# Another order of products and of VectorE's and ScalarE's work where the gate and up projections in blocks pass to the down projection

## The chip, the cores and the metric

The kernel runs on one core of a Trainium2 chip. The metric is the time of one execution in device microseconds (us); the value shown for a kernel is the median of its runs. A profile of one further execution gives, for every instruction, engine, start, duration and what it waited for. The engines are named as the profile names them: PE is TensorE, DVE is VectorE, ACT is ScalarE, POOL is GpSimd, SP is SyncE.

## The reference

One inference layer for a prompt of 512 tokens and 8 samples of 8 tokens that share all weights. A mixer (an SSD scan and an mLSTM scan) and a cross attention come first; the last block is the feed-forward part, where the change lies:

```python
u = _rms(x) * g_pre_ffn
f = (jax.nn.silu(u @ w_gate) * (u @ w_up)) @ w_down
x = x + _rms(f) * g_post_ffn
```

All is float32. The width is 1024, the hidden width 2816, that is 22 tiles of 128; the 576 tokens are worked on together.

## The kernel before, in words

**Products of float32 in three.** Every float32 operand is kept as a high part (rounded to a shorter format) and a low part (the rest). A product of 128 by 128 weights with an operand is three matmuls: high by high, high by low, low by high (L1735 to L1737, and L1941, L1942, L1939 for the down projection). The high part is a cast on ScalarE, the low part a subtraction on VectorE, or for some weights a copy with a negative sign on ScalarE and an accumulating transfer on POOL's queue (L1879 and L1880, L1675 and L1676).

**Blocks.** From hidden tile 4 on, gate and up are taken two hidden tiles at a time (class `Pair`, one for gate and one for up), over two halves of the 1024 features and two halves of 288 tokens. That is a 2 by 2 by 2 block product, done with seven block products instead of eight. Block product `w` (0 to 6) multiplies a sum of weight blocks (`factor`) with a sum of input blocks (`b11`, `b21`, `b22`, `parts(1)` to `parts(4)`) in 12 matmuls of 128x288. Products 0, 2, 4 and 5 add up in one PSUM bank `x`, and after each of 0, 2 and 4 the sum so far is copied out by ScalarE before the next is added: to the first half of `cc`, to `ct[:, 0]`, to the second half of `cc` (`c3`). Products 1, 3 and 6 have banks of their own (`y`, `z`), and VectorE adds a copied sum to them. `early` does 0 and 1, `mid` does 2, 3 and 4, `late` does 5 and 6. `done` (L1740) finishes one output block: a gate block gets its SiLU on ScalarE (L1746) behind an addition on VectorE where one is needed (L1745); an up block is multiplied with its gate block (L1750, L1752) and then goes to `place`.

**The operand of the down projection.** The down projection is a block product too (class `Down`, four pairs of output tiles, 0 to 3, in each pass). Its inputs are `hop`, seven combinations of the four hidden blocks `g11`, `g12`, `g21`, `g22`, numbered 0 to 6, each with a high part (cast, L192 or L1770) and a low part (subtraction, L193 or L1773). Three combinations need one block each (0, 1 and 2); the other four come from differences of blocks (`minus`, L1621) when the last block is there.

**The passage.** `down_blocks(c, up_gate, j)` runs twice, for hidden tiles 4 to 9 and 10 to 15. It holds the last gate pair `g_` (products 5 and 6 open), the last up pair `u` and the four `Down` objects. Its list of events `on(t, step)` is sorted by `t`, and that sorted list is the order of instructions on every engine: each engine takes its own instructions one after the other, and an instruction that waits holds those behind it on that engine. Around the passage `u`'s products 0 and 1 come first, then `g_`'s 5 and 6, then `u`'s 2, 3 and 4, then product 0 of `Down` 0, then `u`'s 5 and 6, and then the rest of `Down` 0: products 1, 3, 2 and 5 first for the two older hidden pairs (`(0, 1)`), then for the newest (`(2,)`).

Between them on VectorE and ScalarE stand the weight sums of `Down` 0 and 1: `sum1`, `sum2`, `diff1`, `diff2` on VectorE (L1891 and L1621), `high1` to `high4` as casts (L1885, L1904, L1914, L1922), `low1v` and `low2` to `low4` as subtractions (L1907); `low1` of the third and fourth pair by ScalarE and POOL (L1879, L1880). `keep` copies a down bank to `cc` or `ct` (L1945), `plus` adds it to another on VectorE (L1948), `store` sends rows to memory over POOL's queue (L1954). The matmuls of a down product in the trace read `hop` and weights that are called `whi`, `wlo`, `wacc`, `u3h` or `u3l` after the buffer that they lie in. There are 3 buffers each of `whi` and `wlo`, so a new cast waits for the last product that reads the old weights.

## Time and profile before

| | us |
|---|---|
| median of 3 runs | 1112.37 |
| lowest and highest run | 1111.8 and 1116.81 |
| the profiled execution | 1110.66 |
| its span, first to last instruction | 1108.9 |
| PE busy in the span | 1093.2 |
| DVE, ACT busy in the span | 772.8 and 605.1 |
| first pass through the changed passage | about 839 to 865 of the span |
| second pass | about 942 to 968 |

Times in the views count from the start of the span. A row of the view in order of time has the start, the duration, the engine, the line, the operation, the tile written and the tiles read, and in brackets how long the engine was idle before it and which instruction ended that. A matmul's duration includes its way through the array, so matmuls overlap: distances of their starts show the pace. A row of waits has total, times and longest.

### The profile page before, as it was taken

How to read it: one execution, taken by the hardware profiler on the slowest of the kernel's cores; microseconds unless marked ns; L12 is line 12 of the kernel's file. 1: busy time of each engine (PE TensorE's matmuls, PEld its weight loads, DVE VectorE, ACT ScalarE, POOL GpSimd, SP SyncE). 2: the span in 40 equal slices, each digit the busy share in tenths (PEclk: the TensorE clock that was granted, in tenths of full speed). 3: DMA queues.
4: the chain of work that ended last, by engine and by line, in shares of the span. 5: the costliest groups of instructions: out<-in, count | busy, mean ns of one | idle time of the engine just before them, and what ended most of it. 6: DMA issues, size and time to landing. Idle time of an engine off the chain costs nothing.

```text
span 1108.9 us, 21249 instructions
## 1 busy us (share of the span) xinstructions
PE 1093.2 (99%) x8355; PEld 1041.6 (94%) x8355; DVE 772.8 (70%) x1521; ACT 605.1 (55%) x1122; POOL 217.2 (20%) x301
## 2 busy tenths in 40 slices
PE   9999999999999999999999999999999999999997
PEld 8999889898998999999988889999999999999997
DVE  6796775558785785568744456676578879888655
ACT  6867533246563466656534445635565556556654
POOL 1332542323121121110134301100000210020000
PEclk9999999999999999999999999999999999999999
DMA  6785553435473437873487755652552863397432
GB/s 208 172 155 129 137 160 124 156 84 160 127 207 105 119 136 269 267 257 104 143 271 285 265 184 165 225 183 55 184 147 79 200 163 90 84 240 215 104 135 86
DMA packets 59432, 182.34 MB, mean 164 GB/s; under 512 B 6556, under 2 KB 10780, under 8 KB 58820
## 3 DMA queue, kind: packets, MB, share of 16 engines
q1 hardware_dynamic: 44324, 142.19, 39.1%
q0 software_dynamic: 14720, 38.28, 16.4%
q8 instruction: 65, 1.06, 0.4%
q10 hardware_dynamic: 288, 0.52, 0.1%
q14 instruction: 35, 0.29, 0.1%
HBM read 151.66 MB, written 29.30 MB: 163 GB/s over the span
## 4 chain that ended last, share of the span: by engine, by line
PE 82%; DVE 5%; ACT 4%; DMA 4%; issue 1%; POOL 0%; DVEq 0%; ACTq 0%; SPq 0%; POOLq 0%
PE ps_in L201 5%; PE ps_in L202 5%; PE ps_in L203 5%; PE ps_g L1735 3%; PE ps_g L1736 3%; PE ps_g L1737 3%; PE ps_u L1735 2%; PE ps_u L1736 2%; PE ps_u L1737 2%; PE ps_o L201 2%; PE ps_o L203 2%; PE ps_o L202 2%; PE ps_dn L201 2%; PE ps_dn L203 2%; PE ps_dn L1942 2%; PE ps_dn L202 2%
## 5 line engine op out<-in xcount | busy, mean ns | idle before, releaser
L201 PE MATMUL ps_in<-uh,whi 128*128 128x320 f32 (+1 forms) x544 | 164.5, 303 | 1.4 <-DVE cb L426 1.2
L203 PE MATMUL ps_in<-uh,wlo 128*128 128x320 f32 (+1 forms) x544 | 163.5, 301 | 0.0
L202 PE MATMUL ps_in<-ul,whi 128*128 128x320 f32 (+1 forms) x544 | 163.1, 300 | 0.0
L181 ACT CAST whi<-raw 128x1024 fp32r<-128x1024 f32 (+1 forms) x102 | 102.8, 1012 | 85.3 <-PE ps_in L202 30.1
L188 DVE TENSOR_TENSOR wlo<-raw,whi 128x512 fp32r<-128x512 f32 (+1 forms) x94 | 90.4, 963 | 55.8 <-ACT whi L181 55.1
L201 PEld LDWEIGHTS ps_in<-uh,whi 128*128 128x128 f32 x544 | 103.0, 189 | 4.7 <-issue 1.7
L203 PEld LDWEIGHTS ps_in<-uh,wlo 128*128 128x128 f32 x544 | 103.0, 189 | 1.4 <-issue 0.4
L202 PEld LDWEIGHTS ps_in<-ul,whi 128*128 128x128 f32 x544 | 103.1, 190 | 1.2 <-issue 0.4
L186 POOL DMA_DIRECT2D wlo<-win x32 | 28.0, 885 | 87.5 <-ACT wlo L185 71.5
L1735 PE MATMUL ps_g<-b,whi 128*128 128x288 f32 x144 | 42.7, 297 | 1.2 <-ACT cc L1803 1.0
L1735 PE MATMUL ps_u<-b,whi 128*128 128x288 f32 x144 | 42.8, 297 | 0.0
L1736 PE MATMUL ps_u<-b,whi 128*128 128x288 f32 x144 | 42.5, 295 | 0.0
L1736 PE MATMUL ps_g<-b,whi 128*128 128x288 f32 x144 | 42.5, 295 | 0.0
L201 PE MATMUL ps_o<-mixs_h,whi 128*128 128x320 f32 (+1 forms) x128 | 38.2, 298 | 0.5 <-DVE tmp L991 0.5
L201 PE MATMUL ps_xo<-qh,whi 128*128 128x288 f32 x128 | 37.9, 301 | 0.4 <-ACT whi L181 0.3
L201 PE MATMUL ps_xq<-u2h,whi 128*128 128x320 f32 (+1 forms) x128 | 38.2, 302 | 0.0
L203 PE MATMUL ps_o<-mixm_h,wlo 128*128 128x256 f32 (+1 forms) x128 | 38.2, 298 | 0.0
L202 PE MATMUL ps_xq<-u2l,whi 128*128 128x320 f32 (+1 forms) x128 | 38.0, 298 | 0.0
L201 PE MATMUL ps_o<-mixm_h,whi 128*128 128x256 f32 (+1 forms) x128 | 38.0, 297 | 0.0
L202 PE MATMUL ps_o<-mixm_l,whi 128*128 128x256 f32 (+1 forms) x128 | 37.9, 296 | 0.0
L203 PE MATMUL ps_xq<-u2h,wlo 128*128 128x320 f32 (+1 forms) x128 | 37.9, 296 | 0.0
L202 PE MATMUL ps_o<-mixs_l,whi 128*128 128x320 f32 (+1 forms) x128 | 37.7, 294 | 0.0
(776 smaller groups left out, 3897.7 us busy)
## 6 DMA issues: line engine op xcount, KB each, us to landing
raw<-win SPq DMA_DIRECT2D x35, 512.0 KB, 3.7
raw<-wout SPq DMA_DIRECT2D x17, 512.0 KB, 5.3
kva<-kc SPq DMA_DIRECT2D x16, 512.0 KB, 6.5
kva<-vc SPq DMA_DIRECT2D x16, 512.0 KB, 6.4
raw<-wxq SPq DMA_DIRECT2D x13, 512.0 KB, 3.8
raw<-wgate SPq DMA_DIRECT2D x13, 512.0 KB, 4.4
raw<-wup SPq DMA_DIRECT2D x13, 512.0 KB, 4.3
wlo<-win POOLq DMA_DIRECT2D x24, 256.0 KB, 5.5
```

What stands on the lines that cost most here:

```text
L181: A.copy(hi[:, :n], raw[:, :n])
L186: G.dma_start(lo[:, a:b], src[:, a:b], accum_op=ALU.add)
L188: e.tensor_tensor(lo[:, a:b], raw[:, a:b], hi[:, a:b].bitcast(F32), op=ALU.subtract)
L201: mm(ps, wh, ah, start=i == 0, stop=False)
L202: mm(ps, wh, al, start=False, stop=False)
L203: m = mm(ps, wl, ah, start=False, stop=i == len(tiles) - 1)
L1735: mm(ps, wh, b[0][:, k, :], start=start and k == 0, stop=False, skip_group_check=True)
L1736: mm(ps, wh, b[1][:, k, :], start=False, stop=False, skip_group_check=True)
L1737: m = mm(ps, wl, b[0][:, k, :], start=False, stop=k == 3, skip_group_check=True)
L1942: mm(ps, wh, bl, start=False, stop=False, skip_group_check=True)
```

## The change

Only places change; no arithmetic is added or removed. The product `w = 2` of the last up pair is done between the last gate pair's products 4 and 5 (`up_between`, tied behind product 4 by `issue_after`), not behind 6. The copy of its sum to `ct[:, 0]` is issued inside `done` of the gate block (0, 1), between that block's addition (which reads the old `ct[:, 0]`) and its SiLU; that `done` itself is sorted later, at -3.1, behind `low1v` (-4.2) and `diff1` (-4.1) of `Down` 0. The work behind the up pair's products 5 and 6 is written out in `gate_last` and `place_last`: the gating of block `g21` and its cast come behind product 5 and its low part behind the addition of product 6; the four differences are placed with their casts, and the low parts follow in the order 3, 4, 6, 5. `Down` 0 takes product 5 for the older hidden pairs ahead of product 3 and 1 for the newest, and 3 before 1. `sum2` of `Down` 1 moves from 3.4 to 8.6, `high2` from 8.6 to 8.95, and `low1` of `Down` 2 from 9.6 to 10.5.

```diff
-        def done(s, a, i, ps, more=None):
+        def done(s, a, i, ps, more=None, then=None):
             g = gates(s.j)[a][i]
             if not s.up:
                 if more is not None:
                     V.tensor_tensor(g, ps, more, op=ALU.add)
+                if then:
+                    then()
                 A.activation(g, ps if more is None else g, AF.Silu)
                 return
...
-            s.mul(s.x, 4, parts(3), False)
+            s.m4 = s.mul(s.x, 4, parts(3), False)
...
+        op, ((g11, g12), (g21, g22)) = operand(u.j), gates(u.j)
+        def high(m, g):
+            A.copy(op[:, m, :], g)
+        def low(m, g):
+            V.tensor_tensor(op[:, 7 + m, :], g, op[:, m, :].bitcast(F32), op=ALU.subtract)
+        def gate_last():
+            V.tensor_tensor(g21, g21, u.x, op=ALU.mult)
+            high(1, g21)
+        def place_last():
+            V.tensor_tensor(ct[:, 1, :], u.z, ct[:, 0, :], op=ALU.add)
+            low(1, g21)
+            V.tensor_tensor(g12, g12, ct[:, 1, :], op=ALU.mult)
+            minus(g11, g12, g11)
+            high(3, g11)
+            minus(g12, g22, g12)
+            high(5, g12)
+            low(3, g11)
+            minus(g22, g22, g11)
+            high(4, g22)
+            minus(g21, g21, g22)
+            high(6, g21)
+            low(4, g22)
+            low(6, g21)
+            low(5, g12)
...
-        on(-8.0, up_mul, g_, "x", 5, parts(4), False)
-        on(-6.35, done, g_, 1, 0, "x")
-        on(-6.4, up_mul, g_, "z", 6, b22, False)
-        on(-4.7, lambda: g_.done(0, 1, g_.z, g_.c2))
-        on(-4.8, up_mul, u, "x", 2, parts(2), False)
-        on(-3.15, lambda: A.copy(ct[:, 0, :], u.x))
+        def up_between():
+            with tc.issue_after(g_.m4.ins):
+                up_mul(u, "x", 2, parts(2), False)
+        on(-8.0, up_between)
+        on(-6.4, up_mul, g_, "x", 5, parts(4), False)
+        on(-4.75, done, g_, 1, 0, "x")
+        on(-4.8, up_mul, g_, "z", 6, b22, False)
+        on(-3.1, lambda: g_.done(0, 1, g_.z, g_.c2, lambda: A.copy(ct[:, 0, :], u.x)))
...
-        on(2.9, done, u, 1, 0, "x")
+        on(2.9, gate_last)
...
-        on(4.5, lambda: u.done(0, 1, u.z, ct[:, 0, :]))
+        on(4.5, place_last)
...
-        on(6.8, mul, 0, "y", 1, 1, (2,))
-        on(7.2, mul, 0, "z", 3, 3, (2,))
-        on(7.6, mul, 0, "w", 5, 6, (0, 1), True, False)
+        on(6.8, mul, 0, "w", 5, 6, (0, 1), True, False)
+        on(7.6, mul, 0, "z", 3, 3, (2,))
+        on(8.0, mul, 0, "y", 1, 1, (2,))
...
-        for k, p in (("sum1", 2.3), ("high1", 2.85), ("sum2", 3.4), ("low1v", 8.7), ("high2", 8.6), ("low2", 9.6), ("diff1", 9.7),
+        for k, p in (("sum1", 2.3), ("high1", 2.85), ("sum2", 8.6), ("low1v", 8.7), ("high2", 8.95), ("low2", 9.6), ("diff1", 9.7),
...
-            a_ = ((9.6, 12.2), (18.0, 20.6))[n_ - 2]
+            a_ = ((10.5, 12.2), (18.0, 20.6))[n_ - 2]
```

In the changed kernel the lines from L1746 to the new part of `down_blocks` lie 2 further on (L1907 is L1909 there), and the new functions and events have lines from L2004 to L2054. Three places of the order, in the first pass. The first is TensorE behind the gate pair's product 4 (rows of the change with a +); `b_8940` is where `parts(1)` and `parts(2)` lie, `b_8835` where `parts(3)` and `parts(4)` do:

```order
 L1736 MATMUL ps_g<-b_8835,whi 128x288
 L1737 MATMUL ps_g<-b_8835,u3l 128x288
+L1735 MATMUL ps_u<-b_8940,whi 128x288
+L1736 MATMUL ps_u<-b_8940,whi 128x288
+L1737 MATMUL ps_u<-b_8940,wlo 128x288
```

The three new rows stand four times: the up pair's product 2 now stands between the gate pair's 4 (`u3l`) and 5. The second place is VectorE around the gate block's addition, before:

```order
L193 TENSOR_TENSOR hop_9999<-gt,hop_9999 128x288
L1907 TENSOR_TENSOR wacc<-rawx,wacc 128x768
L1745 TENSOR_TENSOR gt<-ps_g,ct 128x288
L1907 TENSOR_TENSOR wlo<-raw,whi 128x768
L1773 TENSOR_TENSOR hop_9710<-gt,hop_9710 128x288 x2
L1621 TENSOR_TENSOR raw<-raw,sw 128x384
```

and with the change, with ScalarE's rows of the same stretch behind it:

```order
L193 TENSOR_TENSOR hop_9946<-gt,hop_9946 128x288
L1909 TENSOR_TENSOR wacc<-rawx,wacc 128x768
L1909 TENSOR_TENSOR wlo<-raw,whi 128x768
L1775 TENSOR_TENSOR hop_9710<-gt,hop_9710 128x288 x2
L1621 TENSOR_TENSOR raw<-raw,sw 128x384
L1745 TENSOR_TENSOR gt<-ps_g,ct 128x288
```

```order
L1772 CAST hop_9710<-gt 128x288
L1887 CAST whi<-raw 128x768
L192 CAST hop_9946<-gt 128x288
L1916 CAST wacc<-rawx 128x768
L1748 ACTIVATE gt<-ps_g 128x288
L1772 CAST hop_9710<-gt 128x288 x2
L2046 COPY ct<-ps_u 128x288
L1748 ACTIVATE gt<-gt 128x288
L1924 CAST u3h<-raw 128x3x128
```

On VectorE the addition L1745 now stands behind `wlo` (`low1v`), two `hop` rows and `raw` (`diff1`). On ScalarE one `hop` cast has moved ahead of `whi` and one SiLU behind `wacc`, and the copy to `ct` (L2046) stands ahead of the last SiLU. The third place is VectorE from the gating of block `g21` on, before:

```order
L1752 TENSOR_TENSOR gt<-gt,ps_u 128x288
L193 TENSOR_TENSOR hop_9999<-gt,hop_9999 128x288
L1621 TENSOR_TENSOR sw<-sw,raw 128x384
L1750 TENSOR_TENSOR ct<-ps_u,ct 128x288
L1752 TENSOR_TENSOR gt<-gt,ct 128x288
L1621 TENSOR_TENSOR gt<-gt 128x288 x2
L1773 TENSOR_TENSOR hop_9999<-gt,hop_9999 128x288
```

and with the change:

```order
L2013 TENSOR_TENSOR gt<-gt,ps_u 128x288
L2017 TENSOR_TENSOR ct<-ps_u,ct 128x288
L2010 TENSOR_TENSOR hop_9946<-gt,hop_9946 128x288
L2019 TENSOR_TENSOR gt<-gt,ct 128x288
L1621 TENSOR_TENSOR gt<-gt 128x288 x2
L2010 TENSOR_TENSOR hop_9946<-gt,hop_9946 128x288
L1621 TENSOR_TENSOR gt<-gt 128x288 x2
L2010 TENSOR_TENSOR hop_9946<-gt,hop_9946 128x288 x3
L1621 TENSOR_TENSOR sw<-sw,raw 128x384
L1909 TENSOR_TENSOR wlo<-raw,whi 128x768
```

The low part of combination 1 (the `hop` row) has gone behind the addition L2017, the differences stand two and two, and `sw` (`sum2` of `Down` 1) stands behind the last low part.

## The prediction

> **What bounds the kernel now.** I read the page's busy shares first, then TensorE's list of waits, then TensorE's instructions in order of time through the stretch that the change touches, then the chain of waits there. The first fence holds the span, TensorE's busy row, and two rows of TensorE's waits (total us, times, longest).

> ```profile
> span 1108.9 us, 21249 instructions
> PE 1093.2 (99%) x8355; PEld 1041.6 (94%) x8355; DVE 772.8 (70%) x1521; ACT 605.1 (55%) x1122; POOL 217.2 (20%) x301
> ...
> PE ps_g L1735 <- ACT cc L1803: 1.0, 2, 0.5
> PE ps_dn L1941 <- ACT hop L1770: 0.8, 2, 0.4
> ```

> TensorE is busy all the time, so an edit of order can only win what TensorE waits. Both rows say "2 times": the two passes through `down_blocks` look alike, and I work out the first and double it. TensorE's own rows there (start, duration, line, [idle before <- who ended it]):

> ```profile
> 840.76 0.29 PE L1737 MATMUL ps_g<-b,u3l 128*128 128x288 f32 x1
> 841.53 0.40 PE L1735 MATMUL ps_g<-b,whi 128*128 128x288 f32 x1 [0.49 <-ACT cc L1803]
> 841.77 0.30 PE L1736 MATMUL ps_g<-b,whi 128*128 128x288 f32 x1
> ...
> 842.97 0.29 PE L1736 MATMUL ps_g<-b,whi 128*128 128x288 f32 x1
> ...
> 843.23 0.29 PE L1735 MATMUL ps_g<-u3h 128*128 128x288 f32 x1
> ...
> 844.81 0.29 PE L1735 MATMUL ps_u<-b,whi 128*128 128x288 f32 x1
> ...
> 848.01 0.40 PE L1735 MATMUL ps_u<-b,whi 128*128 128x288 f32 x1
> ...
> 850.89 0.40 PE L1735 MATMUL ps_u<-b,whi 128*128 128x288 f32 x1
> ...
> 854.16 0.29 PE L1941 MATMUL ps_dn<-hop,whi 128*128 128x288 f32 x1
> ...
> 856.80 0.29 PE L1939 MATMUL ps_dn<-hop,wlo 128*128 128x288 f32 x1
> 857.49 0.40 PE L1941 MATMUL ps_dn<-hop,whi 128*128 128x288 f32 x1 [0.40 <-ACT hop L1770]
> ...
> 861.08 0.29 PE L1941 MATMUL ps_dn<-hop,wacc 128*128 128x288 f32 x1
> ```

> A product of 12 matmuls takes 844.81 - 843.23 = 1.58, so starts are 0.132 apart. Against that pace: 840.76 to 841.77 holds two steps, 1.01 - 0.26 = 0.75 lost. The starts at 848.01 and 850.89 also show 0.40 instead of 0.29, about 0.1 lost each. From 856.80 to 861.08 there are 19 steps, 4.28 - 2.50 = 1.78 lost. Sum **2.7 per pass, 5.5 in both**: the ceiling of any gain is 0.5%.

> The chain of waits (start, its time on the chain, engine, tile, line) tells who is late in the second stall:

> ```profile
> 844.47 0.33 ACT hop L192
> 844.80 0.31 ACT gt L1746
> 845.11 0.73 ACT wacc L1914
> 845.86 0.96 DVE wacc L1907
> 846.82 0.37 DVE gt L1745
> 847.19 0.87 DVE wlo L1907
> 848.05 0.74 DVE hop L1773 x2
> 848.79 0.48 DVE raw L1621
> ...
> 855.62 0.38 DVE ct L1750
> ...
> 857.47 0.47 DVE hop L1773
> ```

> From 845.86 on it is VectorE's queue: TensorE finished the up pair's last product near 854.2, VectorE took it up (L1750) only at 855.6.

> **First stall: removed.** The change puts the up pair's product 2 between the gate pair's 4 and 5, so ScalarE's copy of `cc` is covered. Product 2 goes from 840.89 to 842.47, with its inputs long there. Product 5 runs 842.47 to 844.05, product 6 to 845.63, the up pair's 3 to 847.21. The 0.75 is won, and TensorE arrives at the up pair's product 4 at **847.21** instead of 848.01.

> **What product 4 waits for: the new stall.** Product 4 adds into the bank that must first be copied to `ct`. That copy is now issued behind the gate pair's last addition (L1745), which reads the same part of `ct`. In VectorE's order L1745 has gone from before the weight difference `wlo` to behind `wlo`, two `hop` differences and `raw`. The head of that queue moves as well:

> ```profile
> 843.30 0.84 ACT L1885 CAST whi<-raw 128x768 fp32r<-128x768 f32 x1 [0.52 <-PE ps_g L1736]
> ...
> 845.01 0.82 ACT L1914 CAST wacc<-rawx 128x768 fp32r<-128x768 f32 x1
> ...
> 847.57 0.38 ACT L2012 COPY ct<-ps_u 128x288 f32<-128x288 f32 x1
> ```

> ScalarE's cast `whi` starts 0.33 after the last high product of 5 (842.97), whose weight buffer it takes. That product is now at 842.47 + 1.33 = 843.80, so `whi` starts at 844.13. Before, `wacc` came 1.71 later with three short operations between; now one stands between (two of about 0.32 moved), so 1.07 later: 845.20, done 846.02. VectorE then, with the chain's pieces: `wacc` 846.06, `wlo` 847.02, two `hop` 847.89, `raw` 848.63, L1745 at 849.1, done 849.5; the copy (0.38) is done 849.9; product 4 starts at **849.95**. Cost: 849.95 - 847.21 = 2.7 idle and 0.1 of a slow restart. The term is 0.2 smaller if `wacc` starts as early as before (845.86); its other bound, no wait at all, is rival A. Queued behind the copy on ScalarE: the SiLU of gate part (0,1), then the casts `u3h` and `whi`, which VectorE waits for; their lateness is in what follows. SP's order is untouched: its two loads behind `u3l` go out about 1 later, and their first reader, ScalarE's `wlo`, is itself 4 later (rival B).

> **Second stall: mostly gone.** From product 4 to the up pair's 5 is 850.89 - 848.01 = 2.88, so 852.83; here the copy of the bank is covered by the down product, and the 0.1 is saved. From 5 to the down products, 854.16 - 850.89 less 0.11 = 3.16: **855.99**, 1.83 later than before. VectorE now finds the last up product when it ends: with 0.3 from a last matmul to its reader, the addition that was at 855.53 to 855.62 is at 856.15, only 0.6 later. `low(1)` goes into the 0.5 that VectorE spent waiting for its own result, about 0.4 more. The differences then come near 857.4, 857.85, 858.65, 859.1, with casts 0.45 behind each; the lows of 3, 4, 6 and 5 are done near 858.75, 860.05, 860.5 and 860.9. TensorE now has 24 matmuls on the two older operands first (the old order had 18, and then needed parts 1 and 3): 855.99 + 3.16 = 859.15 before it needs part 3, which is there, and part 4 at about 859.9, 0.1 to 0.2 short. I take 0.35 with restarts, in place of 1.78; it lies between 0.1 and 0.8 (one more VectorE operation late).

> **Third: a stall that is not there now.** `sum2` of the second down pair (128x384, on VectorE at 855.06 now) moves behind the last low, to about 860.8. All that hangs on it follows late:

> ```profile
> 862.01 0.56 DVE L1621 TENSOR_TENSOR raw<-raw,sw 128x384 f32<-128x384 f32 x1
> ...
> 863.02 0.71 ACT L1945 COPY cc<-ps_dn 128x288 f32<-128x288 f32 x2
> ...
> 863.44 0.82 DVE L1948 TENSOR_TENSOR fst<-cc,ps_dn 128x288 f32<-128x288 f32 x2 [0.88 <-ACT cc L1945]
> ...
> 864.26 0.30 PE L1941 MATMUL ps_dn<-hop,u3h 128*128 128x288 f32 x1
> ```

> The product at 864.26 reuses the bank that the VectorE addition at 863.44 (done 863.9) reads: 0.37 to spare. After the change: `sum2` done 861.35, ScalarE's cast 862.2, its difference on VectorE 863.45, `raw` 863.95 (now 862.57), the cast `u3h` 864.45, the copy `cc` 864.8, the addition done 865.3. TensorE gets there at 864.26 + 0.35 = 864.6. So 0.65 and a restart: **0.75**; from below 0 (if the copy to `cc` does not have to sit behind `u3h`), from above 1.5 (1.4 later, `raw`'s own shift).

> **Sum.** After: 2.8 + 0.35 + 0.75 = 3.9 lost a pass, now 2.7: **+1.2 a pass, +2.4 in both**. The profiled execution took 1110.66 (span 1108.9 and 1.76 around it), so 1113.1; the median shown is 1112.37, 1.7 above that execution, so 1114.8 on its scale.

> **Rivals.** *A, product 4 is not held:* VectorE reaches L1745 before 847.2. Then only the restarts, 0.35 and nothing later remain of 2.7: -2.3 a pass, 1107.7. For it: TensorE's first stall surely goes. Against: in this trace L1745 ran at 846.82 with `wlo`, `hop` and `raw` (2.1) still behind it, and these are ahead of it now; I see no slack. 5%.

> *B, a late transfer; the slower side.* ScalarE's `wlo` (L1879) moves behind the late copy of `cc`, from 860.4 to 864.7, and POOL's accumulating load of the third down pair's weights waits for it, with a store queued behind it on POOL.

> ```profile
> 861.57 0.86 POOL L1880 DMA_DIRECT2D wlo<-wdown  x1 [23.43 <-ACT wlo L1879]
> ...
> DMA to landing us min/median/max: 4.9/5.6/6.3
> ...
> 870.98 0.56 PE L1939 MATMUL ps_dn<-hop,wlo 128*128 128x288 f32 x3
> ...
> f_d<-gt POOLq DMA_DIRECT2D x3, 288.0 KB, 7.8
> ```

> Issue would be at 865.85, landing at 870.75 to 872.15; it is needed at 870.98 + 1.2 = 872.2. Up to 6.3 it is hidden; with the 7.8 that POOL's stores show, it is 1.45 late: +2.65 a pass, 1117.7, and 0.15 more makes it slower by half a per cent. It decides from 6.35 us on. 9%.

> *C, the clock.* A stall of 2.7 is longer than any here; if the granted clock halved after it, product 4 and the down product behind it (2.88) would take twice that: +4.1 a pass, 1120.6. The longest wait of now, and the next four us:

> ```profile
> 355.87 0.64 PE L911 MATMUL ps_nh<-c,qpad 128*32 128x257 f32 x8 [1.68 <-DMA c<-c]
> ...
> 356.40:360.40 4.00, 4.00 (x36) 3.96 (x33) 3.83 (x11) 0.62 (x3) 0.68 (x1) 1.00 0.75 185
> ```

> After 1.68 idle the clock column still reads 1.00, so I give it 3%. [...]

> **How the numbers follow.** The forecast has 83%: 1114.8. Its own range, from the ends above, is +0.2 (third stall absent, `wacc` early) to +2.4 a pass (third at 1.5, second at 0.8), 1112.8 to 1117.2. Runs of one kernel differ here by some us (1111.8 to 1116.81), and B lies just above, so 1110.5 to 1118.3; A and C are left out. Half a per cent, about what a measurement of this kernel can tell from no change, is 5.6: even A is not faster by that much. Faster 2%, same 88%, slower 10% (half of B, C, and the forecast's upper edge).

> **What would show it.** In the changed profile: no wait of L1735 for the `cc` copy at the gate pair's product 5; instead L1735 of the up pair waiting over 2 us for ScalarE's copy of `ct`, with L1745 just ahead on VectorE, twice. The waits of down products for ScalarE's `hop` cast gone or under 0.2. A wait of some 0.6 in front of the down product with `u3h`, for VectorE's addition. If product 4 starts by 848, the sum is wrong by 2 a pass and A holds; if TensorE waits for POOL's load of `wlo`, B; a clock under 0.95 in the slice behind the stall, C.

## The result and the profile after

| | before | after |
|---|---|---|
| median of 15 runs each, taken side by side (us) | 1115.29 | 1120.29 |
| lowest and highest run | 1111.8 and 1120.38 | 1117.04 and 1125.55 |
| ratio after to before, 95% interval | | 1.0057 [1.0045, 1.007] |
| span of the profiled execution | 1108.9 | 1120.2 |
| mean granted clock of TensorE in it | 0.998 | 0.994 |

The change made the kernel slower by 0.57%, about 6.3 us. The forecast was 2.4 us more. The two profiled executions differ by 11.3 us, but 4.3 of that lie ahead of the changed passage (the up pair's product 3 issues its last matmul at 851.36 instead of the 847.08 that the forecast's working gives; a stretch with the granted clock at 0.50 from 356.8 on is part of it), so I compare stretches and not spans.

TensorE's list of waits in the changed kernel (total us, times, longest) has the stall that was forecast, and two smaller ones:

```profile
PE ps_u L1735 <- ACT ct L2046: 5.2, 2, 2.6
...
PE ps_dn L1941 <- DMA wlo<-wdown: 0.8, 1, 0.8
...
PE ps_dn L1943 <- DVE fst L1950: 0.6, 2, 0.3
```

The waits for `cc` at the gate pair's product 5 and for ScalarE's `hop` cast are gone. The chain of waits ahead of the first row is the one that was worked out: the weight difference `wlo`, two `hop` rows and `raw` ahead of the addition L1745, and the copy behind it.

```profile
849.56 0.75 ACT wacc L1916
...
851.20 0.95 DVE wlo L1909
852.15 0.74 DVE hop L1775 x2
852.89 0.47 DVE raw L1621
853.36 0.38 DVE gt L1745
...
853.82 0.41 ACT ct L2046
...
854.27 0.40 PE ps_u L1735
```

What was not worked out stands in TensorE's own rows behind that wait (start, duration, line, what is multiplied):

```profile
851.36 0.29 PE L1737 MATMUL ps_u<-b,wlo 128*128 128x288 f32 x1
854.27 0.40 PE L1735 MATMUL ps_u<-b,whi 128*128 128x288 f32 x1 [2.61 <-ACT ct L2046]
854.50 0.29 PE L1736 MATMUL ps_u<-b,whi 128*128 128x288 f32 x1
...
855.17 0.44 PE L1735 MATMUL ps_u<-b,whi 128*128 128x288 f32 x1
855.40 0.45 PE L1736 MATMUL ps_u<-b,whi 128*128 128x288 f32 x1
855.64 0.45 PE L1737 MATMUL ps_u<-b,u3l 128*128 128x288 f32 x1
...
858.69 0.29 PE L1735 MATMUL ps_u<-b,whi 128*128 128x288 f32 x1
```

851.36 to 854.50 holds two steps of 0.132, so 2.88 are lost, as forecast (2.8). But from 855.17 on, a matmul takes 0.45 instead of 0.29 and starts are 0.24 apart. From 855.17 to 858.69 there are 15 steps: 3.52 instead of 1.98, **1.54 lost with nothing to wait for**. The view by stretches (length, then busy time and instructions of TensorE, its weight loads, VectorE, ScalarE and GpSimd, then granted clock, DMA share, GB/s) says why, in both passes:

```profile
851.80:855.20 3.40, 0.93 (x7) 0.93 (x8) 2.14 (x6) 1.38 (x4) 0.00 (x0) 0.99 0.00 0
855.20:858.60 3.40, 3.40 (x17) 3.40 (x16) 2.22 (x4) 1.17 (x3) 0.00 (x0) 0.50 0.60 181
858.60:862.00 3.40, 3.40 (x28) 3.40 (x28) 1.38 (x3) 1.71 (x4) 0.00 (x0) 1.00 0.13 51
...
957.50:960.90 3.40, 0.88 (x6) 0.89 (x7) 2.14 (x6) 1.34 (x4) 0.00 (x0) 1.00 0.00 0
960.90:964.30 3.40, 3.40 (x17) 3.40 (x16) 2.27 (x4) 1.25 (x3) 0.00 (x0) 0.51 0.56 174
```

The clock is 0.50 for one stretch of 3.4 us behind each wait: 17 matmuls where the next stretch holds 28. That is rival C. The second and third stall:

```profile
865.80 0.29 PE L1943 MATMUL ps_dn<-hop,whi 128*128 128x288 f32 x1
866.08 0.40 PE L1944 MATMUL ps_dn<-hop,whi 128*128 128x288 f32 x1
...
867.16 0.40 PE L1943 MATMUL ps_dn<-hop,wacc 128*128 128x288 f32 x1
867.40 0.29 PE L1944 MATMUL ps_dn<-hop,wacc 128*128 128x288 f32 x1
...
870.71 0.29 PE L1941 MATMUL ps_dn<-hop,wlo 128*128 128x288 f32 x1
871.31 0.40 PE L1943 MATMUL ps_dn<-hop,u3h 128*128 128x288 f32 x1 [0.31 <-DVE fst L1950]
871.55 0.29 PE L1944 MATMUL ps_dn<-hop,u3h 128*128 128x288 f32 x1
```

865.80 to 867.40 holds seven steps, 1.60 - 0.92 = 0.68 lost (forecast 0.35); 870.71 to 871.55 holds two, 0.84 - 0.26 = 0.58 (forecast 0.75). What the second stall is made of stands in the rows of the weight loads (PEld):

```profile
866.08 0.19 PEld L1944 LDWEIGHTS ps_dn<-hop,whi 128*128 128x128 f32 x1 [0.21 <-DVE hop L2010]
...
867.16 0.19 PEld L1943 LDWEIGHTS ps_dn<-hop,wacc 128*128 128x128 f32 x1 [0.29 <-ACT ct L1947]
```

By the steps up to 866.81, 0.35 are lost where TensorE waits for VectorE's low parts, as forecast; the other 0.33, at 867.16 and the start behind it, come from ScalarE's copy of a down bank (L1947, `keep`), which the forecast did not have. So a pass loses 2.88 + 0.68 + 0.58 = 4.1 in stalls (forecast 3.9) and 1.54 in the clock, against 2.7 before: +2.9 a pass. Twice that is 5.9, and the wait for the transfer of `wlo`, which came in the second pass alone, makes it some 6.9 in this execution; 6.3 were measured over the runs.

### The profile page after: what moved, and what is told of

Its sections match the earlier page's. It is cut to its first block, busy times and chain, and to the rows that moved or that the text cites. A ratio compares the mean times of both kernels' runs of the same rounds, so it can differ in the third digit from the quotient of the medians.

```text
span 1120.2 us, 21251 instructions
## 1 busy us (share of the span) xinstructions
PE 1097.5 (98%) x8355; PEld 1045.7 (93%) x8355; DVE 773.0 (69%) x1521; ACT 605.1 (54%) x1122; POOL 216.8 (19%) x301
## 3 DMA queue, kind: packets, MB, share of 16 engines
q8 instruction: 65, 1.06, 0.4%
## 4 chain that ended last, share of the span: by engine, by line
PE 74%; DMA 8%; DVE 5%; ACT 5%; issue 3%; POOL 1%; DVEq 0%; ACTq 0%; POOLq 0%; SPq 0%
PE ps_in L201 5%; PE ps_in L202 5%; PE ps_in L203 5%; PE ps_u L1735 3%; PE ps_u L1736 3%; PE ps_u L1737 3%; PE ps_g L1735 3%; PE ps_g L1736 3%; PE ps_g L1737 3%; PE ps_v L774 2%; PE ps_v L772 2%; PE ps_v L773 2%; PE ps_dn L201 2%; PE ps_dn L203 2%; PE ps_dn L202 2%
## 5 line engine op out<-in xcount | busy, mean ns | idle before, releaser
L1735 PE MATMUL ps_u<-b,whi 128*128 128x288 f32 x144 | 43.2, 300 | 5.2 <-ACT ct L2046 5.2
L1736 PE MATMUL ps_u<-b,whi 128*128 128x288 f32 x144 | 43.1, 300 | 0.0
L1735 PE MATMUL ps_g<-b,whi 128*128 128x288 f32 x144 | 42.5, 296 | 0.2 <-ACT cc L1794 0.2
L1736 PE MATMUL ps_g<-b,whi 128*128 128x288 f32 x144 | 42.5, 295 | 0.0
L202 PE MATMUL ps_xo<-ql,whi 128*128 128x288 f32 x128 | 37.7, 295 | 0.0
```

What stands on the lines that cost most here:

```text
L202: mm(ps, wh, al, start=False, stop=False)
L1735: mm(ps, wh, b[0][:, k, :], start=start and k == 0, stop=False, skip_group_check=True)
L1736: mm(ps, wh, b[1][:, k, :], start=False, stop=False, skip_group_check=True)
```

## The experiments

Every ratio is to the kernel before, from runs side by side on the same chip. The word "pass" is as in the prediction; "lost" is time beyond 0.132 per start on TensorE.

**1. Fill the wait.** The changed kernel, with 18 products ahead of the up pair's product 4 whose results are thrown away. TensorE still gets to product 4 when the copy is done, but is busy until then.

```diff
+        def fill():
+            bank(0, "w")
+            for _ in range(18):
+                mm(ds[0].w, b11[0][:, 0, 0:128], b11[0][:, 0, :], start=True, stop=True, skip_group_check=True)
+        on(-1.65, fill)
```

> The changed kernel with 18 extra matmuls of 128x288, whose results are thrown away, in front of the up pair's product 4 in both passes. They fill the wait for the copy of ct with TensorE work and leave every wait as it is. Theory (the long idle stretch makes the granted clock drop, and the half clock after it is what was not in the forecast): no slice at half clock behind the wait, product 4 starts where it did, and the kernel is 1.4 us a pass, some 2.9 us in all, faster than the changed kernel; against the kernel before it is still 2.5 to 3.5 us slower. Rival (the clock is not tied to this wait, or the missing time lies elsewhere): the clock drops all the same and the time is that of the changed kernel, 5 to 6.5 us slower than before.

Measured: 1.0014 [1.0005, 1.0022], against 1.0057 [1.0045, 1.007]. TensorE's rows (18 throw-away matmuls, then product 4):

```profile
849.09 2.53 PE L2051 MATMUL ps_dn<-u3h 128*128 128x288 f32 x18
...
851.86 0.40 PE L1735 MATMUL ps_u<-b,whi 128*128 128x288 f32 x1 [0.24 <-ACT ct L2046]
```

and the stretch behind them, with 31 matmuls and the clock at 1.00:

```profile
852.00:856.00 4.00, 4.00 (x31) 4.00 (x32) 2.71 (x5) 2.42 (x6) 0.00 (x0) 1.00 0.43 135
```

Counted from the last matmul of product 3, product 4 starts as late as without the filling (2.9 in both), yet the kernel is 0.43% (4.8 us) faster; between the ends of the two intervals, 2.6 to 7.2. The two half-clock stretches are worth 3.1 and the transfer of `wlo`, which was not late here, 1.0. So the clock is the larger part of what the forecast lacked.

That does not rest on the profiled executions alone, since every run has its mean granted clock on record. Over the 15 runs of the changed kernel it is 0.9957 on average, over the 11 of this experiment 0.9984, and over the 23 runs of the kernel before beside them 0.9984 too. One stretch of 3.41 us at half clock, as from 855.16 to 858.58 and from 960.98 to 964.39 in the profiled execution of the changed kernel, takes 0.0015 off the mean of a run. So the changed kernel has some 1.8 such stretches more in a run, at 1.54 each 2.7 us. Its two fastest runs (1117.04 and 1117.13) are the two with the highest clock, 0.998.

What the stalls alone cost is then 1.0014, 1.6 us (0.6 to 2.5 by the interval), where the forecast said 2.4. The expectation, 2.5 to 3.5 slower than before, was missed: the rows of this execution lose 1.4 a pass more than before, 2.8 in both, and why the runs show less is open.

**2. Put the addition back.** The changed kernel with one number undone: the gate block's addition with the copy behind it goes ahead of `wlo` again.

```diff
-        on(-3.1, lambda: g_.done(0, 1, g_.z, g_.c2, lambda: A.copy(ct[:, 0, :], u.x)))
+        on(-4.7, lambda: g_.done(0, 1, g_.z, g_.c2, lambda: A.copy(ct[:, 0, :], u.x)))
```

> The changed kernel with one number put back: the last gate block's addition, with the copy of ct behind it, is sorted at -4.7 again, ahead of low1v and diff1 on VectorE. Theory (this place alone makes the 2.6 us wait, and with it the clock drop): product 4 waits 0.6 instead of 2.6 in both passes, no half clock behind it, and the kernel is 5.5 to 7 us faster than the changed kernel; against the kernel before it is between 1 us faster and 0.5 us slower, because the wait of some 0.5 in front of the down product that reads u3h stays. Rival (the wait has another root, such as the later whi cast on ScalarE): product 4 still waits over 1.5 us, and the clock drops in some of the passes.

Measured: 0.9998 [0.9984, 1.0013]. TensorE's waits in the first pass:

```profile
851.81 0.40 PE L1735 MATMUL ps_u<-b,whi 128*128 128x288 f32 x1 [0.54 <-ACT ct L2046]
855.03 0.40 PE L1735 MATMUL ps_u<-b,whi 128*128 128x288 f32 x1 [0.16 <-ACT cc L2049]
```

The 2.61 has become 0.54 and the clock stays at 1.00 in both passes: with this one number put back, the time can't be told from that of the kernel before.

**3. Put `sum2` back.** The changed kernel with `sum2`, `high2` and `low1` in their old places.

```diff
-        for k, p in (("sum1", 2.3), ("high1", 2.85), ("sum2", 8.6), ("low1v", 8.7), ("high2", 8.95), ...
+        for k, p in (("sum1", 2.3), ("high1", 2.85), ("sum2", 3.4), ("low1v", 8.7), ("high2", 8.6), ...
-            a_ = ((10.5, 12.2), (18.0, 20.6))[n_ - 2]
+            a_ = ((9.6, 12.2), (18.0, 20.6))[n_ - 2]
```

> The changed kernel with sum2, high2 and low1 at their old numbers (3.4, 8.6, 9.6). Theory (these set the wait in front of the down product that reads u3h, and the late transfer of wlo from POOL's queue): both waits go, 0.5 us a pass and up to 0.8 us for the transfer, 1 to 2 us in all against the changed kernel, and the 2.6 us wait and the half clock stay. Against the kernel before 4 to 5 us slower. Rival (these waits are only passed on): the same time as the changed kernel, with a new wait at the down products for ScalarE or VectorE.

Measured: 1.0047 [1.0033, 1.0062]. The waits for L1950 and for the transfer of `wlo` are gone, the one for `ct` is still 5.2 in two, and both stretches at a clock of 0.50 are there (from 855.23 and 961.04). The third stall is gone from the rows, but the 1.1 us between this ratio and that of the change are within the noise of both, so the runs don't show what it is worth. It is not the cause of the loss.

**4. How long must a wait be?** The kernel before, with a measuring stretch behind its end: 40 casts on ScalarE of eight lengths in turn, each of which TensorE waits for and then issues 66 to 86 matmuls of 128x288. None of it enters the output.

```diff
+    lens = (800, 1240, 1680, 2100, 2540, 2970, 3400, 4050)
+        for n_ in range(40):
+            A.copy(dst[:, 0:lens[n_ % 8]], src[:, 0:lens[n_ % 8]])
+            ps = GP("ps_map")[:, :288]
+            for _ in range(66 + 5 * (n_ // 8)):
+                mm(ps, dst[:, 0:128], dst[:, 0:288], start=True, stop=True, skip_group_check=True)
```

> The kernel before with a measuring stretch behind its end: 40 times a ScalarE copy that TensorE must wait for, of eight lengths from 800 to 4050 columns (TensorE idle for about 1 to 4 us), each followed by 66 to 86 matmuls of 128x288 without a pause. The stretch adds work, so only its rows are read, not the time. Theory (the clock is judged in fixed stretches of some 3.4 us that run freely, and one with too little work is followed by one at half clock): idle times of 1.8 us and less never halve the clock, 2.6 us does so in some or most cases by where the stretch falls, over 3.4 us always; each half-clock part is about 3.4 us long whatever the idle time. Rival (a fixed idle time sets it off, and the slow part starts with the first matmul): one sharp bound between 1.7 and 2.6 us and slow matmuls from the restart on.

TensorE's rows, one for each wait: start, time of the group of matmuls, their number, the wait. The third round (76 matmuls: 10.28 at full clock) and three rows of the fifth (86: 11.59):

```profile
1317.69 10.28 PE L2324 MATMUL ps_map<-hl 128*128 128x288 f32 x76 [1.37 <-ACT hl L2321]
1329.70 10.27 PE L2324 MATMUL ps_map<-hl 128*128 128x288 f32 x76 [1.74 <-ACT hl L2321]
1342.06 11.81 PE L2324 MATMUL ps_map<-hl 128*128 128x288 f32 x76 [2.08 <-ACT hl L2321]
1356.32 11.81 PE L2324 MATMUL ps_map<-hl 128*128 128x288 f32 x76 [2.45 <-ACT hl L2321]
1370.94 12.97 PE L2324 MATMUL ps_map<-hl 128*128 128x288 f32 x76 [2.81 <-ACT hl L2321]
1387.08 11.82 PE L2324 MATMUL ps_map<-hl 128*128 128x288 f32 x76 [3.17 <-ACT hl L2321]
...
1569.10 11.59 PE L2324 MATMUL ps_map<-hl 128*128 128x288 f32 x86 [2.08 <-ACT hl L2321]
1583.14 11.60 PE L2324 MATMUL ps_map<-hl 128*128 128x288 f32 x86 [2.45 <-ACT hl L2321]
...
1613.84 11.59 PE L2324 MATMUL ps_map<-hl 128*128 128x288 f32 x86 [3.17 <-ACT hl L2321]
```

A drop cost 1.54 here (11.81 for 10.27), whatever the wait, or less where its stretch began before the matmuls did, and more only where two half-clock stretches followed each other (12.97 for 10.27, 2.7). Over all rounds: none of 14 waits of 1.00 to 1.74 dropped the clock, 2 of 5 of 2.08, 4 of 5 each of 2.45, 2.81 and 3.17, and all 5 of 3.71. Length alone didn't decide: 2.45 and 3.17 stand there both ways. The starts of the drops lie on one grid with a period of 3.413 us: the first at 1151.65, the last at 1629.52, 140 periods of 3.4133 apart, and those between on it to 0.01 us. I call one period a cell. If each wait is cut at that grid, the largest piece in one cell parts the cases cleanly: 20 waits with at most 1.78 in one cell left the clock up, 19 with 1.91 or more dropped it (the expectations of experiment 6 give these counts as 16 and 22; that was a miscount). So in this execution, among dense matmuls of 128x288, every wait that left 1.91 us or more of one cell empty was followed by a cell at half clock, and none that left at most 1.78.

**5. Leave half the wait.** As experiment 1, with 8 throw-away products, so that a wait of 1.56 stays, which is under the 1.78 of experiment 4 wherever the cells lie.

```diff
-            for _ in range(18):
+            for _ in range(8):
```

> The changed kernel with 8 throw-away matmuls of 128x288 (into the bank that the first down product clears afterwards) ahead of the up pair's product 4, where the run before had 18. They take about 1.06 of the 2.6 us that TensorE waits there, so about 1.5 us of idle time stay, in one piece. The arithmetic that counts is that of the changed kernel. Theory (the clock halves only where a stretch of 3.4 us holds more than about 2 us of idle time): no half clock behind product 4 in either pass, matmul starts 0.132 apart, and the time of the kernel with 18 (ratio to before 1.0005 to 1.0022). Rival 1 (any idle time of some length there does it, or the fill hid something else than the clock): half clock behind product 4 as in the changed kernel, ratio near 1.0057. Rival 2 (it depends on where the free-running stretch lies): one pass halves and the other not, ratio near 1.003.

```profile
849.80 1.21 PE L2051 MATMUL ps_dn<-u3h 128*128 128x288 f32 x8
852.57 0.40 PE L1735 MATMUL ps_u<-b,whi 128*128 128x288 f32 x1 [1.56 <-ACT ct L2046]
```

Both passes have this wait, and the profile shows a clock of 1.00 behind both. The mean granted clock over the 12 runs is 0.9981, against 0.9957 for the change and 0.9986 for the 35 runs of the kernel before beside them, so the half-clock cells are absent from most runs too. The time is 1.0027 [1.001, 1.0044]. That is above the range expected (1.0005 to 1.0022), though the interval is wide and overlaps with that of experiment 1; where the difference comes from is open.

**6. The same wait, at known places in the cells.** Three executions of the changed kernel with eight waits of 3.7 behind its end, whose drops mark the grid; the second has 3 throw-away products, which leave 2.21 of the wait, and the third has 72 matmuls behind each marker. The casts and products behind the end enter no output; each of the three is one execution, and their times are not compared.

```diff
+    lens = (4050,) * 8
+        for n_ in range(8):
+            A.copy(dst[:, 0:lens[n_ % 8]], src[:, 0:lens[n_ % 8]])
+            ps = GP("ps_map")[:, :288]
+            for _ in range(66 + 5 * (n_ // 8)):
+                mm(ps, dst[:, 0:128], dst[:, 0:288], start=True, stop=True, skip_group_check=True)
```

> The changed kernel with eight waits of 3.7 us behind its end (a ScalarE cast of 4050 columns that TensorE waits for, then 66 matmuls of 128x288 whose result is thrown away). Each of them is meant to drop the clock, so that the starts of the half-clock stretches show where the free-running stretches of 3.413 us lie in this execution. Theory (the clock halves for the next stretch where one stretch holds more than about 1.85 us in which TensorE has nothing to do: in the measuring stretch all 16 waits with at most 1.78 us in one stretch left it up, all 22 with at least 1.91 dropped it): counted back from the markers, in each of the two passes the wait of 2.61 at the up pair's product 4 drops the clock if at least 1.91 of it lie in one stretch, and leaves it up if at most 1.78 do; over all places, about 7 in 10. Rival (the length of the wait alone decides, and 2.6 always drops it): half clock in both passes wherever the stretches lie.

> As the run before, with 3 throw-away matmuls of 128x288 ahead of the up pair's product 4, so that about 2.2 us of wait stay in one piece. Theory: at least 1.91 in one stretch of 3.413 drops the clock, at most 1.78 leaves it up (over all places about 4 in 10 drop). Rival (the length alone decides): both passes alike, with or without a drop, wherever the stretches lie.

> As the first of these three, with 72 matmuls behind each marker instead of 66: another execution, in which the stretches lie elsewhere. Theory and rival as there: what lies in one stretch decides in each pass, against half clock in both passes.

In each of the three executions the half-clock stretches of the passes and of the markers fit one grid of 3.413 us, and the three grids lie differently (edges at 855.68, 853.30 and 854.08). The second is the telling one. Both passes wait 2.21:

```profile
853.71 0.40 PE L1735 MATMUL ps_u<-b,whi 128*128 128x288 f32 x1 [2.21 <-ACT ct L2046]
957.81 0.40 PE L1735 MATMUL ps_u<-b,whi 128*128 128x288 f32 x1 [2.21 <-ACT ct L2046]
```

The stretches of the next view are cells of the grid, for each pass the one with the wait and the one behind it:

```profile
849.89:853.30 3.41, 1.61 (x13) 1.37 (x11) 3.28 (x6) 0.84 (x4) 0.00 (x0) 1.00 0.00 0
853.30:856.71 3.41, 3.00 (x22) 3.00 (x23) 2.06 (x4) 2.24 (x5) 0.00 (x0) 1.00 0.20 29
955.70:959.11 3.41, 1.30 (x10) 1.30 (x11) 2.13 (x5) 1.75 (x4) 0.00 (x0) 1.00 0.00 0
959.11:962.52 3.41, 3.41 (x17) 3.41 (x16) 2.41 (x5) 1.27 (x4) 0.00 (x0) 0.50 0.69 213
```

In the first pass the cell's edge at 853.30 cuts the wait (851.50 to 853.71) into 1.80 and 0.41: no drop. In the second all of 955.70 to 957.81, 2.11, lies in one cell: half clock. In the two others the pieces are 2.10, 1.92, 2.61 and 2.61, and all four passes dropped. The rival, that length alone decides, has fallen. Behind the markers a second cell stayed at half clock where 0.68 us (the first execution) or more of the wait reached into it, but not with 0.57 (the second) or less. A wait of 2.61 that fills more than 1.91 of one cell leaves at most 0.70 for the next, and in none of the nine passes at half clock on record did a second cell follow.

**7. The products alone.** The kernel before with the up pair's product 2 between the gate pair's 4 and 5, the addition and copy in their old place on VectorE, the tail as before.

```diff
...
+        on(-8.0, up_between)
+        on(-6.4, up_mul, g_, "x", 5, parts(4), False)
+        on(-4.75, done, g_, 1, 0, "x")
+        on(-4.8, up_mul, g_, "z", 6, b22, False)
+        on(-4.7, lambda: g_.done(0, 1, g_.z, g_.c2, lambda: A.copy(ct[:, 0, :], u.x)))
```

> The kernel before with the first part of the change alone: the up pair's product 2 between the gate pair's products 4 and 5, with the copy of its sum behind the addition of block (0, 1), which stays where it was on VectorE (ahead of the weight difference and the two hop rows). The tail behind the up pair's products 5 and 6 and the weight sums stay as before. Theory (what TensorE wins at the gate pair's product 5 it gives back at the first down products, since VectorE's queue sets their start): the 0.75 at product 5 is gone, product 4 waits 0.5 to 0.8 for the copy to ct, the wait of the down products for ScalarE's hop cast stays near 1.8: 0 to +0.5 a pass, ratio 0.999 to 1.001. Rival (the order of products is a gain by itself, and only the later addition spoils it): 0.75 a pass faster, ratio 0.9985 or less.

Measured: 1.0003 [0.999, 1.0016].

```profile
854.30 0.40 PE L1735 MATMUL ps_u<-b,whi 128*128 128x288 f32 x1 [0.54 <-ACT ct L2017]
857.52 0.40 PE L1735 MATMUL ps_u<-b,whi 128*128 128x288 f32 x1 [0.17 <-ACT cc L2020]
864.13 0.40 PE L1943 MATMUL ps_dn<-hop,whi 128*128 128x288 f32 x1 [0.40 <-ACT hop L1772]
```

The 0.75 at the gate product comes back at the up products (1.0 more lost there than before), and the down products wait for `hop` as before: in this order VectorE and ScalarE set the pace through the passage, and an earlier TensorE waits for them further on. The rival's gain (0.9985 or less) lies outside the interval.

**8. The tail alone.** The kernel before with the new order behind the up pair's products 5 and 6 (`gate_last`, `place_last`, the first down pair's products 5, 3, 1), all else as before.

```diff
...
+        on(2.9, gate_last)
...
+        on(4.5, place_last)
...
+        on(6.8, mul, 0, "w", 5, 6, (0, 1), True, False)
+        on(7.6, mul, 0, "z", 3, 3, (2,))
+        on(8.0, mul, 0, "y", 1, 1, (2,))
```

> The kernel before with the last part of the change alone: gating of block g21, differences and low parts in the new order and the first down pair's products 5, 3 and 1 in the new order; the up pair's product 2, the addition of block (0, 1) and the weight sums (sum2, high2, low1) stay as before. Theory: the first stall (0.75 and restarts) stays, the second falls from 1.78 to 0.5 to 0.9 a pass, no third: 0.8 to 1.2 a pass less, ratio 0.998 to 0.999. Rival (VectorE is short of time there whatever the order, so the stall moves on to a later down product): within 0.3 a pass of before, ratio 0.9995 to 1.0005.

Measured: 0.9992 [0.9976, 1.0007]. Counted over all of a pass, as here and in the next two, 2.1 are lost instead of 2.8 (2.7 at the three places of the prediction): the second stall falls from 1.78 to 0.9, the first is there as before. That is the theory's direction, a little less than its 0.8 to 1.2, and the time can't be told from no change.

**9. What each part can give.** The changed kernel with gate product 6 directly behind 5, the addition ahead of `wacc` on VectorE, and `sum2`, `high2` and `low1` in their old places.

```diff
-        on(-4.75, done, g_, 1, 0, "x")
-        on(-4.8, up_mul, g_, "z", 6, b22, False)
-        on(-3.1, lambda: g_.done(0, 1, g_.z, g_.c2, lambda: A.copy(ct[:, 0, :], u.x)))
+        on(-5.58, done, g_, 1, 0, "x")
+        on(-5.6, up_mul, g_, "z", 6, b22, False)
+        on(-5.55, lambda: g_.done(0, 1, g_.z, g_.c2, lambda: A.copy(ct[:, 0, :], u.x)))
...
```

> The changed kernel with two of its numbers undone and one step moved earlier: the gate pair's product 6 stands directly behind product 5, the addition of block (0, 1) with the copy to ct stands ahead of the weight difference wacc on VectorE, and sum2, high2 and low1 have their places of before. It is meant to keep what each part can give: no stall at gate product 5, none or under 0.3 at the up pair's product 4, a second stall of 0.5 to 0.9, no third. Theory (the parts add up): 1 to 2 a pass less than before, ratio 0.996 to 0.9985. Rival (VectorE's queue sets the start of the down products, so an earlier TensorE only waits longer there): the second stall grows to 1.5 or more, ratio 0.9985 to 1.0005.

Measured: 0.9989 [0.9976, 1.0001], which can't be told from no change. A pass loses 2.1 instead of 2.8, so the theory's 1 to 2 less was missed, and the time lies in the rival's range. But the rival's mechanism isn't there either: the second stall is 0.9 and not 1.5. Product 4 no longer waits; what was not expected is a wait of product 5, with ScalarE's queue ahead of it showing its cause:

```profile
852.60 0.83 ACT L1906 CAST whi<-sw 128x768 fp32r<-128x768 f32 x1
853.33 0.39 ACT L2049 COPY cc<-ps_u 128x288 f32<-128x288 f32 x1
...
853.78 0.40 PE L1735 MATMUL ps_u<-b,whi 128*128 128x288 f32 x1 [0.53 <-ACT cc L2049]
```

The copy that the up pair's product 5 waits for stands behind a cast that nothing needs before the down products.

**10. The copy ahead of the cast.** Experiment 9 with that copy ahead of `whi`, block (1, 1)'s two VectorE operations ahead of `wlo`, and the block's low part behind it.

```diff
-        on(0.02, lambda: A.copy(c3, u.x))
-        on(0.1, done, u, 1, 1, "z", c3)
+        def gate_22():
+            V.tensor_tensor(ct[:, 1, :], u.z, c3, op=ALU.add)
+            V.tensor_tensor(g22, g22, ct[:, 1, :], op=ALU.mult)
+            high(2, g22)
+        on(-1.55, lambda: A.copy(c3, u.x))
+        on(-0.75, gate_22)
+        on(-0.65, low, 2, g22)
```

> The kernel of the run before (gate product 6 directly behind 5, the addition of block (0, 1) ahead of wacc, weight sums in their old places) with one more move: ScalarE's copy of the second half of cc stands ahead of the cast whi, VectorE's two operations of block (1, 1) stand ahead of the weight difference wlo and the low part of that block behind it. In the run before, the up pair's product 5 waited 0.53 for that copy (0.80 lost a pass) behind the cast of 0.83. Theory: that wait goes, and since VectorE's queue moves up by as much (the block's two operations no longer stand behind wlo), the second stall stays near 1.0: 0.7 a pass less, 1.4 in all, ratio to before 0.9965 to 0.9985. Rival (VectorE's queue sets the start of the down products whatever TensorE does before): the second stall grows by what the first lost, ratio as in the run before, 0.9976 to 1.0001.

Measured: **0.9969 [0.9955, 0.9982]**, faster than before by 3.5 us, and by the two ratios some 10 less than the change. A pass loses 1.3 instead of 2.8; no wait of over 0.25 is left in it. What remains is the second stall, at 0.76, in part VectorE's low parts and in part ScalarE's copy of a down bank (L1947).

## Why the prediction was wrong, point by point

The step that failed is the clock: the prediction left it out of its sum, at 3%, and it came in both passes of the profiled execution, with 1.54 us each. The stalls that the sum was made of came close to their forecast.

- **First stall removed**: right. It is not in the list of waits.
- **What product 4 waits for**: right in cause, order and size: 2.78 and 0.10 lost, forecast 2.7 and 0.1. Experiment 2 shows the place of L1745 as the cause.
- **Second stall**: 0.68 instead of 0.35, inside the range given for it (0.1 to 0.8). The wait for the low parts alone is 0.35, as forecast. The other 0.33, the wait for ScalarE's copy L1947, was left out, although the stall before had one like it (L1945, some 0.28 lost at 860.58).
- **Third stall**: right: VectorE's addition (L1950) ahead of the product with `u3h`, 0.58 for the forecast 0.75.
- **Sum of the stalls**: +1.4 a pass for the forecast +1.2. That the second was 0.33 too small and the third 0.17 too large, so that the sum comes out better than its terms, is luck. Experiment 1, where these stalls are there and the clock stays up, lands at +1.6 us for the forecast +2.4.
- **Rival B**: the transfer was late once in two passes. It took up to 7.6 from issue to landing, where the trace before showed at most 6.3, and cost 1.0. It decided nothing by itself.
- **Rival C, the failed step.** The prediction gave the halved clock 3%, because "after 1.68 idle the clock column still reads 1.00". The step from there to a stall of 2.7 that leaves the clock up was wrong twice. One wait of 1.68 says nothing of one of 2.7: the border of experiment 4, 1.78 to 1.91 in one cell, lies between them. And the row was one draw. The same line in the same stretch of the changed kernel's execution reads:

```profile
356.40:360.40 4.00, 3.83 (x22) 3.17 (x23) 2.89 (x6) 0.51 (x2) 0.92 (x1) 0.57 0.78 185
```

  There the clock did fall, after a wait of 1.94 at that place; after 2.08 in the run of experiment 1 it did not. In the 13 profiled executions whose clock at that place is on record it fell there in seven, after waits of 1.59 to 1.94. The half clock at the end of the execution before starts at 1105.35; if it starts on an edge, as the one at the end of the changed kernel's execution does (1117.99, 46 periods behind 960.98), then 220 periods of 3.4133 before it an edge lies at 354.41 and cuts the 1.68 (354.19 to 355.87) into 0.22 and 1.46. So the row that the 3% rests on shows, by this count, a wait that an edge had cut. My estimate from the grid, with 1.85 taken between the 1.78 and 1.91 of experiment 4: a wait of 2.61 that can begin anywhere escapes only if an edge leaves less than 1.85 on both sides, so the edge must fall between 0.76 and 1.85 from its start, 1.09 of 3.413. By that, C had about two chances in three in each pass, not 3%.
- **The price of C** was wrong the other way: +2.88 a pass, from the matmuls of product 4 and the down product taken twice as long. The half clock lasted one cell behind the wait of 2.61, 3.41 us in both passes, and cost 1.54 once per wait. With 68% for each of two passes 2.1 is to be added to the forecast, with both passes 3.1: 1116.9 and 1117.9 on its scale, 4.5 and 5.5 above before. Measured are 5.0 between the medians and 6.3 by the ratio (5.0 to 7.8 by its interval); the late transfer (1.0 in the profiled execution) is the part of the rest that can be named. That 1120.29 itself lies so far above 1114.8 has another half: in the runs side by side the kernel before had 1115.29, 2.9 more than the median that the forecast started from.

## What to carry to other kernels

A wait of TensorE wasn't priced by its length alone here: where 1.91 us or more of it lay in one cell, it cost about another 1.5 behind its end (all 19 such waits of experiment 4, some with a second cell), and at L911 a wait of 1.59 was followed by half clock (experiment 9). That two waits of 1.2 may be cheaper than one of 2.4 is an estimate from this, which no run here tried. Filling a wait that can't be avoided with throw-away products paid here (1.0014 for 1.0057, experiment 1). When a change gathers several small stalls into one long one, look at the granted clock in the stretch behind it, and do not take one execution in which a like wait went unpunished as evidence. And when a product waits for a copy, look at what stands ahead of the copy on its engine and ahead of its reader on the next one: moving operations of 0.8 to 0.95 us that nobody needs yet from in front of it gave 0.8 of the 1.5 us that experiment 10 wins a pass. The new order of the tail, which wins 0.7 by itself (experiment 8), is in both 9 and 10.
